# A hybrid attention and state-space block on one core: the split-precision projections as three 256-column matmuls into one sum instead of a 512-column and a 256-column matmul into two

## The chip, the core and the metric

The kernel runs on one NeuronCore of a Trainium2 chip. The core's engines each work through their own instruction list: TensorE (PE, with its weight loads shown apart as PEld), VectorE (DVE), ScalarE (ACT), GpSimd (POOL) and SyncE (SP), which here only issues transfers. Engines meet through semaphores. The metric is the device time of one execution in microseconds (us). The time before is 1421.0 us, the median of three runs (1420.83 to 1421.26).

## The reference

One layer of a hybrid block on a sequence of 256 tokens of width 2048, all in float32:

```
hn   = rms_norm(x, norm_w)
q, k, v, z_a, z_s, xbc, dt_raw, g_a, g_s = split(hn @ w_in)
o_a  = dilated attention of q, k, v (16 heads of 128)  * silu(z_a)
xbc  = silu(causal_depthwise_conv(xbc, 4 taps) + bias)
xs, B, C = split(xbc)          # 4096, 1024 and 1024 columns
y    = state-space scan(xs, softplus(dt_raw), a, B, C) + d_skip * xs
y    = rms_norm(y * silu(z_s), ssm_norm_w)
out  = x + (sigmoid(g_a) * (o_a @ w_attn_branch)
            + sigmoid(g_s) * (y @ w_ssm_branch)) @ w_out
return rms_norm(out, final_norm_w)
```

`w_in` is 2048 x 22592, `w_ssm_branch` 4096 x 2048, `w_attn_branch` and `w_out` 2048 x 2048: 480 tiles of 512 KB, some 252 MB of weights, each read once.

## The kernel before

**Split precision.** Every large product is made of three products in the matmul type fp32r. A weight tile `w` of 128 x 1024 comes in by one transfer and is split into `h` (ACT, L201) and the rest `l = w - h` (DVE, L203). The activations are split in the same way and stand side by side: `XT[:, kt, :256]` is the high part of 256 tokens for the 128 input features of step `kt`, `XT[:, kt, 256:]` the low part. `yT0` holds the same before the tokens' norm factor is known. The product is high x high plus high x low plus low x high.

**Two forms of the product.** In `gemm_b` (gates, v, the branch projections and the last product; L306 to L308) the activations are the stationary operand and 512 weight columns move through the array: three matmuls of 512 columns into one sum for each step and token half. In `gemm_a` (L240, L243) and `gemm_first` (L264, L265) the weights are stationary, 128 x 128, and the tokens move. There `h` is multiplied with all 512 columns of `XT[:, kt, :]`, so that one PSUM bank holds high x high in its first 256 columns and high x low in the last 256, and `l` is multiplied with the 256 high columns and added to the last 256. A projection of 128 output features takes 16 such steps. Three quarters of `w_in`'s columns go this way: the state-space inputs B, C, xs and their gate zs (here called the SSM stage, 31 + 31 + 7 + 7 projections after the first four, which `gemm_first` makes together), `dt` (64 output features wide) and q, k, za of the 16 heads (the attention stage, 48 projections).

**Evacuation.** `evac` (L268) adds the two halves: ACT copies the last 256 columns to SBUF (L270), DVE adds the first 256 from PSUM (L272, or L274 with a factor 0.5). The result goes through the convolution (`conv`: ACT for one tap and the bias, L440, DVE for three taps, L442) and `half_silu` (ACT tanh L280, DVE L281), or straight to q and k. The very first projections (B, C, x, z of group 0 and dt) are made from `yT0` and have to be multiplied with the tokens' factor `rx` afterwards (L276, L398). `rx` comes from ACT's sums of squares (L373), POOL's power (L320), DVE's diagonal (L329), two matmuls that spread it over the partitions (L330) and a DVE copy (L528). The four banks of tag `g` serve all these sums in turn.

**What sets the order.** A scheduler lays out each engine's list at build time. The splitting of weights has high priority; small work (decays, transposes, scan, scores) is put off by `after` and called by `tick` once in each projection, between its first `h` matmul and the next one. One queue, SP's, issues all weight transfers in the order of use.

Of the kernel before, what the change touches and what calls it, by code (L numbers as in the profile page):

```python
# [148 lines left out]
def hybrid_block(ctx: ExitStack, tc: tile.TileContext, wall, xt, x, pk_d, cst_d, fw_d, out):  # L149
# [24 lines left out]
    sel = cst[:, 1408:1536]  # L174
    nw, dsk = pk[:, 256:288], pk[:, 288:320]
    gp.memset(half, -0.5)

    def bank(tag, bufs, name):
# [27 lines left out]

    def split(src, hi, lo, scale=1.0):
        ac.activation(hi, src, AF.Copy, scale=scale)
        if isinstance(scale, float):
# [20 lines left out]
    def gemm_a(tag, xs_of, n_kt=KT, width=P):  # L230
        name = f"{tag[0]}{tag[1]}"
        acc = bank("g", 4, f"ps_{name}") if width == P else bank("m1", 2, f"ps_{name}")
        first = FIRST[tag]
        uk = UNIT // width
        for u in range(n_kt // uk):
            h, l = unit(first + u, (uk, width))
            for kk in range(uk):
                kt = u * uk + kk
                m = xs_of(kt)
                pe.matmul(acc[:width], h[:, kk, :], m, start=(kt == 0), stop=False)  # L240
                if kt == 0:
                    tick()
                pe.matmul(acc[:width, S:], l[:, kk, :], m[:, :S], start=False, stop=(kt == n_kt - 1))  # L243
        return acc

# [3 lines left out]
    def gemm_first(tag, prepare, load_on):  # L249
        name = f"{tag[0]}{tag[1]}"  # L250
        accs = [bank("g", 4, f"ps_{name}_{j}") for j in range(4)]
        for u in range(KT // UB):
            if u % 2 == 0:
                tick()
            for kk in range(UB):
                prepare(u * UB + kk)
            h, l = unit(FIRST[tag] + u, (UB, 512))
            load_on(u)
            for kk in range(UB):
                kt = u * UB + kk  # L260
                m = yT[0][:, kt, :]
                for j, acc in enumerate(accs):
                    js = slice(j * P, (j + 1) * P)
                    pe.matmul(acc, h[:, kk, js], m, start=(kt == 0), stop=False)  # L264
                    pe.matmul(acc[:, S:], l[:, kk, js], m[:, :S], start=False, stop=(kt == KT - 1))  # L265
        return accs

    def evac(acc, out_ap, name, scale=1.0, raw=False):  # L268
        lo = ev.tile([P, S], F32, name=f"lo_{name}", tag="lo", bufs=2)
        ac.activation(lo, acc[:, S:], AF.Copy, scale=scale)  # L270
        if scale == 1.0:
            ve.tensor_tensor(out_ap, acc[:, :S], lo, ALU.add)  # L272
        else:
            ve.scalar_tensor_tensor(out_ap, acc[:, :S], scale, lo, ALU.mult, ALU.add)  # L274
        if raw:
            ve.tensor_tensor(out_ap, out_ap, rx, ALU.mult)  # L276
# [110 lines left out]
    with tc.tile_pool(name="ssm", bufs=2) as sp:  # L387
        def dt_chain(acc):
# [5 lines left out]

            raw, neg, e, z, s, pl, lo, dt, da, ac_t, one = (tmp() for _ in range(11))
# [39 lines left out]
        def conv(acc, ct, out_ap, name, late=False):  # L435
            raw = sp.tile([P, 260], F32, name=f"raw_{name}", tag="raw", bufs=2)
            gp.memset(raw[:, 0:4], 0.0)
            evac(acc, raw[:, 4:], name, raw=late)
            h = ev.tile([P, S], F32, name=f"cv_{name}", tag="eh", bufs=2)
            ac.activation(h, raw[:, 4:], AF.Identity, scale=cw[:, 144 + ct : 145 + ct], bias=cw[:, 192 + ct : 193 + ct])  # L440
            for k in range(3):
                ve.scalar_tensor_tensor(  # L442
                    h, raw[:, 1 + k : 1 + k + S], cw[:, 48 * k + ct : 48 * k + ct + 1], h, ALU.mult, ALU.add
                )
            half_silu(h, out_ap, name)

# [45 lines left out]
        def scan(g, state):  # L492
# [11 lines left out]
            for v, yp in enumerate(yps):  # L504
                u = 2 * g + v
                xs, zs = state["xs"][v], state["zs"][v]
                y1 = sp.tile([P, 2, S], F32, name=f"y1_{u}", tag="y1", bufs=2)
                for i in range(2):
                    t = 2 * u + i
                    ve.scalar_tensor_tensor(  # L510
                        y1[:, i], xs[:, i], dsk[:, t : t + 1], yp[:, i * S : (i + 1) * S], ALU.mult, ALU.add
                    )
                ve.tensor_tensor(y1, y1, zs, ALU.mult)
                ac.activation(xs, y1, AF.Square)
                ve.tensor_tensor(ssq, ssq, xs, ALU.add)
                if u == 8:
                    yT.append(big.tile([P, KT, 2 * S], F32R, name="yT1", tag="yo1"))
                dst = yT[u // 8]
                for i in range(2):
                    t = 2 * u + i  # L520
                    split(y1[:, i], dst[:, t % 16, :S], dst[:, t % 16, S:], scale=nw[:, t : t + 1])

# [4 lines left out]
        with tc.high_priority():  # L527
            ve.tensor_copy(rx, spread(r_x, "x")[:, :S])  # L528
            ve.tensor_scalar(cw, pk[:, 16:256], 0.5, None, ALU.mult)
        for c in range(4):  # L530
            after(1 + 2 * c, lambda c=c: norm_x(c))

        for g in range(GROUPS):
# [12 lines left out]
            for t in range(4 * g, 4 * g + 4):  # L546
# [12 lines left out]
                if i == 0:  # L559
                    state["zs"].append(sp.tile([P, 2, S], F32, name=f"zs{u}", tag="zs", bufs=3))  # L560
                zh = ev.tile([P, S], F32, name=f"zh{t}", tag="eh", bufs=2)
# [8 lines left out]
    with tc.tile_pool(name="att", bufs=2) as ap:  # L570
# [55 lines left out]
        def mix(h, pT, za):  # L626
# [5 lines left out]
            ve.tensor_tensor(o, ops[:, :S], za, ALU.mult)  # L632
            split(o, oaT[:, h, :S], oaT[:, h, S:])

        for h in range(NH):
            q, k = (ap.tile([P, S], F32, name=f"{n}T{h}", tag=f"{n}T", bufs=2) for n in "qk")
            for n, d in (("q", q), ("k", k)):
                evac(project((n, h)), d, f"{n}{h}")
            p = ap.tile([P, 384], F32, name=f"p{h}", tag="p", bufs=2)
# [4 lines left out]
            after(S_LAG, lambda a=(h, q, k, p): scores(*a))  # L644
            zh = ev.tile([P, S], F32, name=f"zah{h}", tag="eh", bufs=2)
            evac(project(("za", h)), zh, f"za{h}", scale=0.5)
            half_silu(zh, za, f"za{h}")

# [92 lines left out]
```

## Time and profile before

| what | value |
|---|---|
| median of three runs | 1421.0 us |
| span of the profiled execution, first to last instruction | 1419.2 us |
| PE busy | 1406.4 us, 99%, 7404 matmul passes |
| DVE busy | 920.5 us, 65% |
| ACT busy | 760.2 us, 54% |
| granted PE clock | 0.999 |
| HBM read | 268.86 MB, 191 GB/s over the span |

The profiled execution's span is 1.8 us below the median of the timed runs, which have a little around the span. A matmul's recorded duration overlaps the next one's, so a matmul's cost on PE is read as the distance from its start to the start of the next, called its slot below. A float32 matmul (not fp32r) shows as two passes.

### The profile page before, as it was taken

What the parts mean: (1) busy time and instruction counts of PE and PEld (TensorE: products, weight loads), DVE (VectorE), ACT (ScalarE), POOL (GpSimd) and SP (SyncE); (2) the same over time, 40 slices, a digit from 0 to 9 for tenths busy, and PEclk for the clock granted to TensorE, in tenths of its full rate; (3) what the DMA queues carried; (4) which work ended last, traced back from release to release, by engine and by line L of the source; (5) the groups of instructions that cost most, each with busy time, mean ns of one, the idle gap of its engine ahead of it and who ended that gap; (6) DMA issues with size and microseconds to landing.
All of it is one profiled execution on the core that took longest, in us unless ns stands there. A gap on an engine that the chain in (4) does not pass through costs nothing.

```text
span 1419.2 us, 19641 instructions
## 1 busy us (share of the span) xinstructions
PE 1406.4 (99%) x7404; PEld 1194.6 (84%) x7404; DVE 920.5 (65%) x1336; ACT 760.2 (54%) x1170; POOL 9.6 (1%) x63
## 2 busy tenths in 40 slices
PE   9999999999999999999999999999999999999997
PEld 7788888888888888888888888888888888888886
DVE  5978888877787888644444446666666654455654
ACT  6656766747575757444533334454544544444443
POOL 0000000000000000000000000000000000000000
PEclk9999999999999999999999999999999999999999
DMA  8566656566656665566566666555555557666663
GB/s 338 183 205 222 197 174 208 169 208 201 189 169 208 194 186 183 167 195 195 187 193 194 192 193 191 176 169 175 170 173 176 168 177 280 193 192 180 191 192 121
DMA packets 77759, 272.31 MB, mean 192 GB/s; under 512 B 8736, under 2 KB 9184, under 8 KB 77024
## 3 DMA queue, kind: packets, MB, share of 16 engines
q1 hardware_dynamic: 77088, 270.01, 60.5%
q8 instruction: 58, 0.95, 0.3%
q10 hardware_dynamic: 576, 1.05, 0.2%
q14 instruction: 37, 0.30, 0.1%
HBM read 268.86 MB, written 2.16 MB: 191 GB/s over the span
## 4 chain that ended last, share of the span: by engine, by line
PE 97%; DVE 1%; issue 0%; DMA 0%; ACT 0%; SPq 0%; POOL 0%; POOLq 0%; DVEq 0%; ACTq 0%
PE ps_xs L240 8%; PE ps_zs L240 8%; PE ps_xs L243 4%; PE ps_q L240 4%; PE ps_zs L243 4%; PE ps_za L240 4%; PE ps_k L240 4%; PE ps_ssm L306 4%; PE ps_ssm L308 4%; PE ps_ssm L307 4%; PE ps_za L243 2%; PE ps_k L243 2%; PE ps_q L243 2%; PE ps_v L306 2%; PE ps_attn L306 2%; PE ps_attn L308 2%
## 5 line engine op out<-in xcount | busy, mean ns | idle before, releaser
L203 DVE TENSOR_TENSOR l<-w,h 128x1024 fp32r<-128x1024 f32 (+1 forms) x481 | 583.1, 1215 | 430.6 <-ACT h L201 428.2
L201 ACT ACTIVATE h<-w 128x1024 fp32r<-128x1024 f32 (+1 forms) x481 | 505.3, 1052 | 573.2 <-PE ps_ssm L308 101.1
L240 PE MATMUL ps_xs<-XT,h 128*128 128x512 f32 x496 | 176.3, 397 | 0.0
L240 PE MATMUL ps_zs<-XT,h 128*128 128x512 f32 x496 | 175.8, 397 | 0.0
L243 PE MATMUL ps_xs<-XT,l 128*128 128x256 f32 x496 | 139.6, 281 | 0.0
L243 PE MATMUL ps_zs<-XT,l 128*128 128x256 f32 x496 | 139.0, 280 | 0.0
L240 PEld LDWEIGHTS ps_zs<-XT,h 128*128 128x128 f32 x496 | 93.1, 188 | 22.6
L240 PEld LDWEIGHTS ps_xs<-XT,h 128*128 128x128 f32 x496 | 93.2, 188 | 22.2
L308 PE MATMUL ps_ssm<-h,yT 128*128 128x512 f32 x256 | 99.6, 389 | 0.0
L307 PE MATMUL ps_ssm<-l,yT 128*128 128x512 f32 x256 | 99.6, 389 | 0.0
L306 PE MATMUL ps_ssm<-h,yT 128*128 128x512 f32 x256 | 99.4, 389 | 0.0
L243 PEld LDWEIGHTS ps_xs<-XT,l 128*128 128x128 f32 x496 | 93.6, 189 | 0.1
L243 PEld LDWEIGHTS ps_zs<-XT,l 128*128 128x128 f32 x496 | 93.6, 189 | 0.0
L240 PE MATMUL ps_q<-XT,h 128*128 128x512 f32 x256 | 90.4, 392 | 0.0
L240 PE MATMUL ps_za<-XT,h 128*128 128x512 f32 x256 | 89.6, 392 | 0.0
L240 PE MATMUL ps_k<-XT,h 128*128 128x512 f32 x256 | 89.6, 391 | 0.0
L243 PE MATMUL ps_q<-XT,l 128*128 128x256 f32 x256 | 74.5, 291 | 0.0
L243 PE MATMUL ps_k<-XT,l 128*128 128x256 f32 x256 | 71.7, 280 | 0.0
L243 PE MATMUL ps_za<-XT,l 128*128 128x256 f32 x256 | 71.7, 280 | 0.0
L240 PEld LDWEIGHTS ps_q<-XT,h 128*128 128x128 f32 x256 | 47.9, 187 | 10.6
L240 PEld LDWEIGHTS ps_k<-XT,h 128*128 128x128 f32 x256 | 47.9, 187 | 10.6
L240 PEld LDWEIGHTS ps_za<-XT,h 128*128 128x128 f32 x256 | 47.9, 187 | 10.6
(235 smaller groups left out, 2553.5 us busy)
## 6 DMA issues: line engine op xcount, KB each, us to landing
w<-in_wall SPq DMA_DIRECT2D x480, 512.0 KB, 3.6
acb<-acum_d SPq DMA_DIRECT2D x32, 256.0 KB, 3.2
th_s<-in_x SPq DMA_DIRECT2D x1, 2048.0 KB, 9.6
fin<-in_x SPq DMA_DIRECT2D x1, 2048.0 KB, 8.1
early<-in_xt SPq DMA_DIRECT2D x7, 256.0 KB, 7.0
fw<-in_fw SPq DMA_DIRECT2D x1, 1024.0 KB, 10.1
out<-fin SPq DMA_DIRECT2D x4, 256.0 KB, 2.9
out<-fin ACTq DMA_DIRECT2D x4, 256.0 KB, 3.2
```

What stands on the lines that cost most here:

```text
L201: ac.activation(h[:, a:b], w[:, a:b], AF.Copy)
L203: eng.tensor_tensor(l[:, a:b], w[:, a:b], h[:, a:b].bitcast(F32), ALU.subtract)
L240: pe.matmul(acc[:width], h[:, kk, :], m, start=(kt == 0), stop=False)
L243: pe.matmul(acc[:width, S:], l[:, kk, :], m[:, :S], start=False, stop=(kt == n_kt - 1))
L306: pe.matmul(accs[i], xh, h, start=(kt == 0), stop=False)
L307: pe.matmul(accs[i], xh, l, start=False, stop=False)
L308: pe.matmul(accs[i], xl, h, start=False, stop=(kt == n_kt - 1))
```

## The change

Each step of a weight-stationary projection becomes three matmuls of 256 columns, `h` with the high tokens, `h` with the low tokens, `l` with the high tokens, all into the same 256 columns of the bank. So there is no second half to add, and `evac` is gone: q and k are one ACT copy from PSUM; the silu gates and the convolution read PSUM directly (ACT once, DVE once or three times); the convolution's zero padding is replaced by shorter taps (253, 254 and 255 columns). The projections of group 0 are multiplied with `rx` straight from PSUM into a `raw` tile. The factor 0.5 that stood in the gate's evacuation moves into the tanh's scale, the norm weights `nwh`, the square and the last split of the attention output.

```diff
@@ gemm_a
-                pe.matmul(acc[:width], h[:, kk, :], m, start=(kt == 0), stop=False)
+                pe.matmul(acc[:width, :S], h[:, kk, :], m[:, :S], start=(kt == 0), stop=False)
                 if kt == 0:
                     tick()
-                pe.matmul(acc[:width, S:], l[:, kk, :], m[:, :S], start=False, stop=(kt == n_kt - 1))
-        return acc
+                pe.matmul(acc[:width, :S], h[:, kk, :], m[:, S:], start=False, stop=False)
+                pe.matmul(acc[:width, :S], l[:, kk, :], m[:, :S], start=False, stop=(kt == n_kt - 1))
+        return acc[:width, :S]
@@ gemm_first
-                    pe.matmul(acc, h[:, kk, js], m, start=(kt == 0), stop=False)
-                    pe.matmul(acc[:, S:], l[:, kk, js], m[:, :S], start=False, stop=(kt == KT - 1))
+                    pe.matmul(acc[:, :S], h[:, kk, js], m[:, :S], start=(kt == 0), stop=False)
+                    pe.matmul(acc[:, :S], h[:, kk, js], m[:, S:], start=False, stop=False)
+                    pe.matmul(acc[:, :S], l[:, kk, js], m[:, :S], start=False, stop=(kt == KT - 1))
...
-    def evac(acc, out_ap, name, scale=1.0, raw=False):
...
-    def half_silu(h, out_ap, name):
+    def silu(src, th_scale, out_ap, name):
         th = ev.tile([P, S], F32, name=f"th_{name}", tag="th", bufs=2)
-        ac.activation(th, h, AF.Tanh)
-        ve.scalar_tensor_tensor(out_ap, th, 1.0, h, ALU.add, ALU.mult)
+        ac.activation(th, src, AF.Tanh, scale=th_scale)
+        ve.scalar_tensor_tensor(out_ap, th, 1.0, src, ALU.add, ALU.mult)
@@ dt_chain
-            ac.activation(lo, acc[:SH, S:], AF.Copy)
-            ve.tensor_tensor(raw, acc[:SH, :S], lo, ALU.add)
-            ve.tensor_tensor(raw, raw, rx[:SH], ALU.mult)
+            ve.tensor_tensor(raw, acc, rx[:SH], ALU.mult)
@@ conv
-            gp.memset(raw[:, 0:4], 0.0)
-            evac(acc, raw[:, 4:], name, raw=late)
+            if late:
+                raw = sp.tile([P, S], F32, name=f"raw_{name}", tag="raw", bufs=2)
+                ve.tensor_tensor(raw, acc, rx, ALU.mult)
+                acc = raw
-            ac.activation(h, raw[:, 4:], AF.Identity, scale=..., bias=...)
+            ac.activation(h, acc, AF.Identity, scale=..., bias=...)
             for k in range(3):
+                d = 3 - k
                 ve.scalar_tensor_tensor(
-                    h, raw[:, 1 + k : 1 + k + S], cw[...], h, ALU.mult, ALU.add
+                    h[:, d:], acc[:, : S - d], cw[...], h[:, d:], ALU.mult, ALU.add
                 )
-            half_silu(h, out_ap, name)
+            silu(h, 1.0, out_ap, name)
@@ zs gate
-                evac(acc, zh, f"z{t}", scale=0.5, raw=t == 0)
-                half_silu(zh, state["zs"][-1][:, i], f"z{t}")
+                silu(acc, 0.5, state["zs"][-1][:, i], f"z{t}")
@@ attention
-                evac(project((n, h)), d, f"{n}{h}")
+                ac.activation(d, project((n, h)), AF.Copy)
...
-            evac(project(("za", h)), zh, f"za{h}", scale=0.5)
-            half_silu(zh, za, f"za{h}")
+            silu(project(("za", h)), 0.5, za, f"za{h}")
```

Over the whole program PE's list grows from 7013 to 9077 rows, DVE's shrinks from 1173 to 1091, ACT's from 1054 to 958, POOL's from 68 to 20, and SP's 531 stay.

How the lists move, at three places. First, PE inside a projection of the SSM stage (`ps_xs` is the sum in PSUM, `XT` the tokens, `h` and `l` the weight parts); before:

```order
L240 MATMUL ps_xs_831<-XT,h_856 128x512 [waits Activation_49]
L243 MATMUL ps_xs_831<-XT,l_857 128x256 [waits DVE_49]
L240 MATMUL ps_xs_831<-XT,h_856 128x512
L243 MATMUL ps_xs_831<-XT,l_857 128x256
L240 MATMUL ps_xs_831<-XT,h_856 128x512
```

and in the change:

```order
L241 MATMUL ps_xs_896<-XT,h_899 128x256 [waits Activation_49]
L244 MATMUL ps_xs_896<-XT,h_899 128x256
L245 MATMUL ps_xs_896<-XT,l_900 128x256 [waits DVE_49]
L241 MATMUL ps_xs_896<-XT,h_899 128x256
L244 MATMUL ps_xs_896<-XT,h_899 128x256
L245 MATMUL ps_xs_896<-XT,l_900 128x256
```

A step of two matmuls has become one of three, in unbroken order.

Second, PE at the start of the first gate projection (`ps_gs`), right behind the dt projection; `rb_x` are the two matmuls that spread the norm factor. Before:

```order
L243 MATMUL ps_dt_352<-yT_84,l_354 64x256
L330 MATMUL rb_x<-diag_x,cst 128x128 [waits DMAHW6_49,DVE_49]
L306 MATMUL ps_gs_0_487<-h_498,yT_84 128x512 [waits PE_49,Activation_49]
L306 MATMUL ps_gs_1_488<-h_498,yT_84 128x512 [waits PE_49]
L330 MATMUL rb_x<-diag_x,cst 128x128 [waits DVE_49]
L307 MATMUL ps_gs_0_487<-l_499,yT_84 128x512 [waits DVE_49]
```

and in the change:

```order
L245 MATMUL ps_dt_417<-yT_85,l_419 64x256
L323 MATMUL rb_x<-diag_x,cst 128x128 [waits DMAHW6_49,DVE_49]
L323 MATMUL rb_x<-diag_x,cst 128x128 [waits DVE_49]
L299 MATMUL ps_gs_0_552<-h_563,yT_85 128x512 [waits DVE_49,Activation_49]
L300 MATMUL ps_gs_0_552<-l_564,yT_85 128x512
L301 MATMUL ps_gs_0_552<-h_563,yT_85 128x512
```

The gate's first matmul now waits for DVE too, and stands behind both matmuls of the norm factor.

Third, DVE in the same place. Before:

```order
L203 TENSOR_TENSOR l_499<-w_273,h_498 128x1024 [waits DMAHW7_49,DVE_49,Activation_49]
L203 TENSOR_TENSOR l_517<-w_514,h_516 128x1024 [waits DMAHW0_49,DVE_49,Activation_49]
L528 COPY rx<-rb_x 128x256 [waits PE_49]
L397 TENSOR_TENSOR early<-ps_dt_352,early 64x256 [waits Activation_49]
L203 TENSOR_TENSOR l_545<-w_542,h_544 128x1024 [waits DMAHW1_49,DVE_49,Activation_49]
L276 TENSOR_TENSOR raw_B_400<-raw_B_400,rx 128x256 [waits DVE_49]
L276 TENSOR_TENSOR raw_C_414<-raw_C_414,rx 128x256
L378 TENSOR_TENSOR early<-early,rx 128x1024 x3
```

and in the change:

```order
L204 TENSOR_TENSOR l_564<-w_314,h_563 128x1024 [waits DMAHW7_49,PE_49,Activation_49]
L521 COPY rx<-rb_x 128x256 [waits PE_49]
L204 TENSOR_TENSOR l_582<-w_579,h_581 128x1024 [waits DMAHW0_49,Activation_49]
L429 TENSOR_TENSOR raw_B_482<-ps_first_0_120,rx 128x256 [waits DVE_49]
L429 TENSOR_TENSOR raw_C_492<-ps_first_1_121,rx 128x256
L389 TENSOR_TENSOR early<-ps_dt_417,rx 64x256
L371 TENSOR_TENSOR early<-early,rx 128x1024 x4
L204 TENSOR_TENSOR l_610<-w_607,h_609 128x1024 [waits DMAHW1_49,Activation_49]
```

The accumulators of B and C (`ps_first_0`, `ps_first_1`) are read for the first time behind `rx`, and the third `l` of the gate has moved from ahead of the token scaling (L378, now L371) to behind all four parts of it.

More of the change, by code (lines that the diff above doesn't have):

```diff
@@ L174, in hybrid_block @@
     sel = cst[:, 1408:1536]
-    nw, dsk = pk[:, 256:288], pk[:, 288:320]
+    dsk = pk[:, 288:320]
     gp.memset(half, -0.5)
+    nwh = lead.tile([P, 32], F32, name="nwh", tag="nwh")
     def bank(tag, bufs, name):
@@ L205, in unit, with split @@
         return h.rearrange("p (k m) -> p k m", k=k), l.rearrange("p (k m) -> p k m", k=k)
-    def split(src, hi, lo, scale=1.0):
-        ac.activation(hi, src, AF.Copy, scale=scale)
-        if isinstance(scale, float):
+    def split(src, hi, lo, scale=None):
+        ac.activation(hi, src, AF.Copy, scale=1.0 if scale is None else scale)
+        if scale is None:
             ve.tensor_tensor(lo, src, hi.bitcast(F32), ALU.subtract)
@@ L263, in gemm_first @@
                     js = slice(j * P, (j + 1) * P)
-                    pe.matmul(acc, h[:, kk, js], m, start=(kt == 0), stop=False)
-                    pe.matmul(acc[:, S:], l[:, kk, js], m[:, :S], start=False, stop=(kt == KT - 1))
-        return accs
-    def evac(acc, out_ap, name, scale=1.0, raw=False):
[L269 to L276, printed above, removed]
-    def half_silu(h, out_ap, name):
+                    pe.matmul(acc[:, :S], h[:, kk, js], m[:, :S], start=(kt == 0), stop=False)
+                    pe.matmul(acc[:, :S], h[:, kk, js], m[:, S:], start=False, stop=False)
+                    pe.matmul(acc[:, :S], l[:, kk, js], m[:, :S], start=False, stop=(kt == KT - 1))
+        return [acc[:, :S] for acc in accs]
+    def silu(src, th_scale, out_ap, name):
         th = ev.tile([P, S], F32, name=f"th_{name}", tag="th", bufs=2)
-        ac.activation(th, h, AF.Tanh)
-        ve.scalar_tensor_tensor(out_ap, th, 1.0, h, ALU.add, ALU.mult)
+        ac.activation(th, src, AF.Tanh, scale=th_scale)
+        ve.scalar_tensor_tensor(out_ap, th, 1.0, src, ALU.add, ALU.mult)
     def gemm_b(tag, x_of, n_kt=KT, held=None):
@@ L393, in tmp @@
                 return dts[:, len(used) - 1, :]
-            raw, neg, e, z, s, pl, lo, dt, da, ac_t, one = (tmp() for _ in range(11))
-            ac.activation(lo, acc[:SH, S:], AF.Copy)
-            ve.tensor_tensor(raw, acc[:SH, :S], lo, ALU.add)
-            ve.tensor_tensor(raw, raw, rx[:SH], ALU.mult)
+            raw, neg, e, z, s, pl, dt, da, ac_t, one = (tmp() for _ in range(10))
+            ve.tensor_tensor(raw, acc, rx[:SH], ALU.mult)
             ve.tensor_scalar(raw, raw, pk[:SH, 320:321], None, ALU.add)
@@ L513, in scan @@
                 ve.tensor_tensor(y1, y1, zs, ALU.mult)
-                ac.activation(xs, y1, AF.Square)
+                ac.activation(xs, y1, AF.Square, scale=0.5)
                 ve.tensor_tensor(ssq, ssq, xs, ALU.add)
@@ L529, in hybrid_block @@
             ve.tensor_scalar(cw, pk[:, 16:256], 0.5, None, ALU.mult)
+            ve.tensor_scalar(nwh, pk[:, 256:288], 0.5, None, ALU.mult)
         for c in range(4):
@@ L560, in hybrid_block @@
                     state["zs"].append(sp.tile([P, 2, S], F32, name=f"zs{u}", tag="zs", bufs=3))
-                zh = ev.tile([P, S], F32, name=f"zh{t}", tag="eh", bufs=2)
-                evac(acc, zh, f"z{t}", scale=0.5, raw=t == 0)
-                half_silu(zh, state["zs"][-1][:, i], f"z{t}")
+                if t == 0:
+                    zr = sp.tile([P, S], F32, name="raw_z", tag="raw", bufs=2)
+                    ve.tensor_tensor(zr, acc, rx, ALU.mult)
+                    acc = zr
+                silu(acc, 0.5, state["zs"][-1][:, i], f"z{t}")
                 if t == 0:
@@ L632, in mix @@
             ve.tensor_tensor(o, ops[:, :S], za, ALU.mult)
-            split(o, oaT[:, h, :S], oaT[:, h, S:])
+            split(o, oaT[:, h, :S], oaT[:, h, S:], scale=0.5)
         for h in range(NH):
```

8 lines of the change are left out of this document (3 added, 5 removed).

## The prediction

> **What bounds the kernel now.** I read the page's first part and the waits of PE first, to see whether PE ever stands still, then PE's timeline, because a busy PE says nothing of how fast it goes.
>
> ```profile
> PE 1406.4 (99%) x7404; PEld 1194.6 (84%) x7404; DVE 920.5 (65%) x1336; ACT 760.2 (54%) x1170; POOL 9.6 (1%) x63
> PE 97%; DVE 1%; issue 0%; DMA 0%; ACT 0%; SPq 0%; POOL 0%; POOLq 0%; DVEq 0%; ACTq 0%
> PE ps_gs L307 <- DVE l L203: 2.1, 3, 1.1
> PE warm L343 <- POOL raw_C L437: 1.3, 1, 1.3
> PE ps_first L264 <- ACT h L201: 1.0, 2, 0.8
> L203 DVE TENSOR_TENSOR l<-w,h 128x1024 fp32r<-128x1024 f32 (+1 forms) x481 | 583.1, 1215 | 430.6 <-ACT h L201 428.2
> ```
>
> PE is busy 99% of the span and 97% of the chain that ended last; in the whole program it waits 4.4 us for others. DVE's largest group sits idle for 430.6 us waiting for ACT, so neither has too much to do. Relief for them can give back at most the waits of PE on them, 2.1 and 1.0 us, both in the first 62 us. So the change is decided by what it does to PE's slots (start to start). Two stretches of the timeline show a step before; columns are start, duration, engine, line, operation.
>
> ```profile
> 1000.21 0.39 PE L240 MATMUL ps_q<-XT,h 128*128 128x512 f32 x1
> 1000.21 0.19 PEld L243 LDWEIGHTS ps_q<-XT,l 128*128 128x128 f32 x1
> 1000.43 0.28 PE L243 MATMUL ps_q<-XT,l 128*128 128x256 f32 x1
> 1000.44 0.19 PEld L240 LDWEIGHTS ps_q<-XT,h 128*128 128x128 f32 x1
> 1000.55 0.39 PE L240 MATMUL ps_q<-XT,h 128*128 128x512 f32 x1
> ...
> 1003.33 0.39 PE L240 MATMUL ps_k<-XT,h 128*128 128x512 f32 x1
> ...
> 101.46 0.40 PE L240 MATMUL ps_zs<-XT,h 128*128 128x512 f32 x1
> 106.66 0.39 PE L240 MATMUL ps_zs<-XT,h 128*128 128x512 f32 x1
> ...
> 400.38 0.40 PE L240 MATMUL ps_zs<-XT,h 128*128 128x512 f32 x1
> 405.69 0.40 PE L240 MATMUL ps_zs<-XT,h 128*128 128x512 f32 x1
> ```
>
> In attention 9 steps take 1003.33 - 1000.21 = 3.12 us, 347 ns each: some 230 for the wide matmul and 117 for the narrow one. In the SSM stage I find two speeds, whole projections long: 15 steps in 5.20 us (347 each, from 101.46) and in 5.31 us (354 each, from 400.38). Most are of the slower kind; I take 352 as the stage's mean. Under each matmul, from its start on, the weights of the next are loaded.
>
> **The change part by part.** *The number of steps:* 76 later SSM projections and 48 of attention have 16 steps each, 1216 and 768; the first four have 64, dt 16; 2064 together, and 2064 matmuls and loads are added. The columns that move stay 768 a step. So the question is what three narrow slots cost against a wide and a narrow one. Two places of this trace answer it from two sides. The first is dt, whose weights are 64 wide:
>
> ```profile
> 29.57 0.39 PE L240 MATMUL ps_dt<-yT,h 128*64 128x512 f32 x1
> 29.79 0.28 PE L243 MATMUL ps_dt<-yT,l 128*64 128x256 f32 x1
> 29.91 0.39 PE L240 MATMUL ps_dt<-yT,h 128*64 128x512 f32 x1
> ...
> 34.67 0.39 PE L240 MATMUL ps_dt<-yT,h 128*64 128x512 f32 x1
> L243 PEld LDWEIGHTS ps_dt<-yT,l 128*64 128x64 f32 x16 | 2.1, 134 | 0.0
> ```
>
> 15 steps in 5.10 us are 340 ns for 768 columns, so 113.3 for each 256 columns: with a short load (134 ns recorded) the slot is the moving alone. That is the lower bound. The other is the start, where four accumulators are fed in turn with full 128-wide weights and narrow matmuls follow one another, as they will everywhere after the change:
>
> ```profile
> 12.27 0.64 PE L265 MATMUL ps_first<-yT,l 128*128 128x256 f32 x4
> 12.75 1.09 PE L264 MATMUL ps_first<-yT,h 128*128 128x512 f32 x4
> 13.68 0.63 PE L265 MATMUL ps_first<-yT,l 128*128 128x256 f32 x4
> 14.15 1.09 PE L264 MATMUL ps_first<-yT,h 128*128 128x512 f32 x4
> 15.08 0.64 PE L265 MATMUL ps_first<-yT,l 128*128 128x256 f32 x4
> ```
>
> Four narrow slots take 0.48 and 0.47 us, 117.5 to 120 each. So a 128-wide load under a narrow matmul isn't hidden whole: it adds 4 to 7 ns to the 113.3. A wide one hides it better: 230 against 226.7 in attention. The change puts three loads where two were, and all three under narrow matmuls. I take 118 a slot, 354 a step, with 117 and 120 (351 and 360) as the ends. The sum lies between +7 and +2 ns a step: attention 768 x 7 = +5.4 us; SSM 1216 x 2 = +2.4; the first four projections 64 x (354 - 350) = +0.3, where 350 is (14.15 - 12.75) / 4; dt 0. Together +8.1 us. At 117 it is 768 x 4 - 1216 x 1 = +1.9, at 120 it is 768 x 13 + 1216 x 8 + 64 x 10 = +20.4.
>
> A rule speaks against the change in another way. The Trainium skill ("TensorE: Matmul & The Clock Gate", section "Back-to-back issue gap") gives a matmul a fixed 2.5 ns beside its columns; two narrow ones for a wide one would then cost 2064 x 2.5 = 5.2 us more. The dt rows don't show it: their wide slot (29.57 to 29.79) and narrow slot (29.79 to 29.91) are as 2 to 1, so by the trace this term is 0 and what counts is the load.
>
> *Is the second load of the same weights saved?* The gates, v and branch projections already use one stationary operand in two matmuls in a row (L306 and L307 both load the high activations):
>
> ```profile
> L307 PEld LDWEIGHTS ps_ssm<-l,yT 128*128 128x128 f32 x256 | 48.1, 188 | 9.9
> L306 PEld LDWEIGHTS ps_ssm<-h,yT 128*128 128x128 f32 x256 | 48.1, 188 | 9.8
> ```
>
> Both are loaded 256 times, 188 ns each; it isn't saved, and I cost it in full. Adding into columns that were written 256 columns ago is nothing new either: before, `l` follows on the last 256 columns of `h`'s bank at that distance.
>
> *Evacuation.* ACT loses a copy and DVE an addition for each projection. This is worth nothing while PE is the bound (above). The sums stay in their bank longer: before until the addition, now until the third tap or the gate's product. With four banks in turn a bank is wanted again three projections later, some 16 x 350 x 3 ns = 17 us. The cover is that DVE and ACT run close behind; gone, PE would stop at a projection's start. I take 0.
>
> *The first gate.* This is the one place where a wait moves, and the order at the second and third place of the change shows it.
>
> ```profile
> 18.42 0.38 SPq L367 DMA_DIRECT2D th_s<-in_x  x1
> th_s<-in_x SPq DMA_DIRECT2D x1, 2048.0 KB, 9.6
> 29.48 0.42 DVE L272 TENSOR_TENSOR raw_C<-ps_first,lo_C 128x256 f32<-128x256 f32 x1
> 29.92 1.91 ACT L373 ACTIVATE th_s<-th_s 128x2048 f32<-128x2048 f32 x1
> 35.36 2.35 DVE L203 TENSOR_TENSOR l<-w,h 128x1024 fp32r<-128x1024 f32 x2
> 36.63 0.50 PE L307 MATMUL ps_gs<-l,yT 128*128 128x512 f32 x1 [0.23 <-DVE l L203]
> 37.63 0.41 DVE L528 COPY rx<-rb_x 128x256 f32<-128x256 f32 x1
> 40.10 3.48 DVE L378 TENSOR_TENSOR early<-early,rx 128x1024 f32<-128x1024 f32 x3
> 46.24 0.50 PE L307 MATMUL ps_gs<-l,yT 128*128 128x512 f32 x1 [1.15 <-DVE l L203]
> 55.45 0.50 PE L307 MATMUL ps_gs<-l,yT 128*128 128x512 f32 x1 [0.76 <-DVE l L203]
> ```
>
> Before, the additions at 29.5 free the two banks and PE is at its third gate matmul at 36.63, so as if it had begun at 36.2. Now the banks come free only with the products by `rx`. ACT no longer has the copies of L270, which wait for PE's last matmul, ahead of its squares, so these can start when `th_s` lands, 18.42 + 9.6 = 28.0, 1.9 us earlier; then PE's last dt matmul at 35.0 sets `rx`, at some 35.7. Behind it come one `l` (1.15) and the first product (0.4): the gate begins at 37.6, 1.4 us late. After that DVE is late with the third `l`, which now stands behind four token scalings (4 x 1.15 = 4.6), and with the fifth, behind ten splits of XT. Walking the list with these durations I get PE waits of 0.5, 2.2 and 0.4 in place of the 1.15, 0.76 and 0.23 shown: 1 us more, +2 us in all, rounded down. Bounds: 0, if DVE's shorter list catches up, and 4.5, if the late start and the new waits come with none of the old ones saved.
>
> The sum: 1419.2 + 8.1 + 2 = 1429.3 us of span; with the 1.8 us that the median lies above the span, 1431 us.
>
> **The rivals.** *Faster: the load hides after all.* If three equal slots let each load end in time, as in dt, a step is 340: -7 x 768 - 12 x 1216 - 10 x 64 = -20.6 us, +2 for the gate, 1402 us. It pays from slots below 116.6 on (the mean step before, 350, divided by 3). For it speaks that the two speeds of the SSM stage look like a matter of how loads and matmuls fall together, which a new rhythm may change. Against it stand the runs of four narrow matmuls at 117.5 to 120. A rule would give it: the Trainium skill, same page, section "LDWEIGHTS (loading the stationary operand)", has 128 columns load in 128 / 1.2 = 107 ns, less than a narrow slot. The narrow slots of 117 with a full load, against 113 with a half one, don't bear that out.
>
> *No change: the repeated weights cost less.* If the middle matmul of a step, whose weights are those in the array, has a 113.3 slot, a step is 349.3: 768 x 2.3 - 1216 x 2.7 = -1.5 us, and with the gate's 2 us about 1421.5. The rows of L306 and L307 say that the load is done, not that it costs the same as any.
>
> *Much slower: PE can't take in a load and a matmul every 118 ns for 1000 us.* Now it takes two pairs in 347. If the pace were 125 a pair, a step would be 375: 768 x 28 + 1216 x 23 + 64 x 25 = +51 us, 1474. Against it: eight transposes in a row at a pair every (1.03 - 0.27) / 7 = 109 ns; but eight are few.
>
> ```profile
> 130.62 1.03 PE L482 MATMUL xtp<-cst,xs 128*128 128x128 f32 x8
> ```
>
> **How the numbers follow.** About 0.2% (2.8 us) is what a measurement of this kernel can tell from no change. My forecast, slots of 117 to 120 and the gate, has 0.67, and its own range is 1423 to 1446; a little of it, at 117 and with no loss at the gate, counts as no change. The repeated-weights rival has 0.13, the hidden load 0.14, the pace 0.06. So faster 0.14, within 0.2% 0.17, slower 0.69. The range that should hold 8 in 10 leaves out the pace and most of the hidden load: 1414 to 1444.
>
> **What would show it.** Right: PE still above 98% busy, the steps of q at 351 to 360 ns, PEld near 9470 loads with 188 each, DVE some 50 us less busy (129 additions of 0.42, as in the row of L272), ACT nearly as much, the first gate beginning near 37.6 us. The hidden load: steps of 340 and PEld rows no shorter. Repeated weights: the slot between L241 and L244 or L244 and L245 shorter than the others. Pace: steps above 365 with gaps put down to issue. Wrong in another way: waits of PE for DVE or ACT at the start of projections, which would mean that banks are held too long.

## The result: 1444.2 us, 1.6% slower

The changed kernel takes 1444.2 us (median of 4 runs, 1444.13 to 1444.30) against 1421.1 us for the kernel before (4 runs beside it). The ratio is 1.016, with a 95% interval of 1.0146 to 1.0175. The forecast was 1431 us with a range of 1414 to 1444: slower was right, the loss is 23 us where 10 were expected, and the time lies 0.2 us above the range. The profiled execution has a span of 1442.4 us and a granted clock of 0.998 (0.999 before).

The page of the changed kernel, its first part and two of its groups (total busy time, then the mean of one in ns):

```profile
PE 1427.5 (99%) x9468; PEld 1308.3 (91%) x9468; DVE 877.4 (61%) x1208; ACT 726.3 (50%) x1073; POOL 6.0 (0%) x15
L204 DVE TENSOR_TENSOR l<-w,h 128x1024 fp32r<-128x1024 f32 (+1 forms) x481 | 584.1, 1216 | 490.4 <-ACT h L202 489.7
L244 PEld LDWEIGHTS ps_xs<-XT,h 128*128 128x128 f32 x496 | 95.2, 192 | 0.1
```

DVE is 43.1 us less busy than before (920.5 - 877.4) and ACT 33.9 us (760.2 - 726.3). Neither gain arrives in the span: DVE's largest group now stands idle for 490.4 us instead of 430.6. PE is still busy 99% of the time, and busy 21.1 us longer. The second matmul of `h` (L244) has its load like any other, 192 ns recorded where the loads of the wide matmul (L240) had 188 before.

PE's slots in attention, timeline of the changed kernel (start, duration, engine, line):

```profile
1000.01 0.28 PE L244 MATMUL ps_q<-XT,h 128*128 128x256 f32 x1
1000.13 0.28 PE L245 MATMUL ps_q<-XT,l 128*128 128x256 f32 x1
1000.25 0.28 PE L241 MATMUL ps_q<-XT,h 128*128 128x256 f32 x1
...
1002.29 0.28 PE L245 MATMUL ps_q<-XT,l 128*128 128x256 f32 x1
```

Nineteen slots take 2.28 us: each is 120 ns, whether the weights are new or those of the matmul ahead. A step is 360 ns. It is so in every projection with 128-wide weights from the SSM stage on, but for the first one or two steps behind other work.

The loss by place, from the starts of the first matmul of each stage. Before:

```profile
82.74 0.39 PE L240 MATMUL ps_xs<-XT,h 128*128 128x512 f32 x1
564.96 0.40 PE L306 MATMUL ps_gs<-h,XT 128*128 128x512 f32 x1
852.76 0.39 PE L240 MATMUL ps_q<-XT,h 128*128 128x512 f32 x1
1143.92 0.58 PE L306 MATMUL ps_ga<-h,XT 128*128 128x512 f32 x1
```

After (with the first and last high matmul of dt):

```profile
30.94 0.28 PE L241 MATMUL ps_dt<-yT,h 128*64 128x256 f32 x1
36.05 0.28 PE L241 MATMUL ps_dt<-yT,h 128*64 128x256 f32 x1
86.09 0.28 PE L241 MATMUL ps_xs<-XT,h 128*128 128x256 f32 x1
578.96 0.40 PE L299 MATMUL ps_gs<-h,XT 128*128 128x512 f32 x1
866.70 0.28 PE L241 MATMUL ps_q<-XT,h 128*128 128x256 f32 x1
1167.30 0.58 PE L299 MATMUL ps_ga<-h,XT 128*128 128x512 f32 x1
```

| stage | later at its end, us | lost in it, us | forecast, us |
|---|---|---|---|
| first four projections (dt began at 29.57) | 1.37 | 1.4 | 0.3 |
| dt and the first gates | 3.35 | 2.0 | 2 |
| SSM stage | 14.0 | 10.65 | 2.4 |
| last gate, v, branch product | 13.94 | -0.1 | 0 |
| attention | 23.38 | 9.4 | 5.4 |
| the rest, to the end of the span | 23.2 | -0.2 | 0 |

The waits of PE at the first gate and the rows around it, changed kernel:

```profile
PE ps_gs L299 <- DVE raw_B L429: 2.1, 1, 2.1
PE ps_gs L300 <- DVE l L204: 1.9, 1, 1.9
```

```profile
29.15 1.91 ACT L366 ACTIVATE th_s<-th_s 128x2048 f32<-128x2048 f32 x1 [3.88 <-DMA th_s<-in_x]
38.51 0.42 DVE L429 TENSOR_TENSOR raw_B<-ps_first,rx 128x256 f32<-128x256 f32 x1
39.08 0.47 PE L299 MATMUL ps_gs<-h,yT 128*128 128x512 f32 x1 [2.07 <-DVE raw_B L429]
52.92 0.50 PE L300 MATMUL ps_gs<-l,yT 128*128 128x512 f32 x1 [1.87 <-DVE l L204]
```

The gate begins when `raw_B` has freed its bank, and loses once more when `l` comes late behind the token scalings. These two stand in place of three smaller waits, and no projection waits for its bank later on.

### The profile page after: what moved, and what is told of

It reads as the page before. It is cut to its first block, busy times and chain, and to the rows that moved or that the text cites. A ratio compares the mean times of both kernels' runs of the same rounds, so it can differ in the third digit from the quotient of the medians.

```text
span 1442.4 us, 23370 instructions
## 1 busy us (share of the span) xinstructions
PE 1427.5 (99%) x9468; PEld 1308.3 (91%) x9468; DVE 877.4 (61%) x1208; ACT 726.3 (50%) x1073; POOL 6.0 (0%) x15
## 4 chain that ended last, share of the span: by engine, by line
PE 97%; DVE 1%; DMA 0%; issue 0%; SPq 0%; ACT 0%; POOLq 0%; DVEq 0%; POOL 0%
PE ps_xs L244 4%; PE ps_xs L241 4%; PE ps_zs L244 4%; PE ps_zs L241 4%; PE ps_zs L245 4%; PE ps_xs L245 4%; PE ps_ssm L299 4%; PE ps_ssm L301 4%; PE ps_ssm L300 4%; PE ps_za L245 2%; PE ps_k L244 2%; PE ps_k L241 2%; PE ps_za L244 2%; PE ps_k L245 2%; PE ps_za L241 2%; PE ps_q L245 2%
## 5 line engine op out<-in xcount | busy, mean ns | idle before, releaser
L204 DVE TENSOR_TENSOR l<-w,h 128x1024 fp32r<-128x1024 f32 (+1 forms) x481 | 584.1, 1216 | 490.4 <-ACT h L202 489.7
L244 PE MATMUL ps_xs<-XT,h 128*128 128x256 f32 x496 | 140.9, 284 | 0.0
L241 PE MATMUL ps_xs<-XT,h 128*128 128x256 f32 x496 | 140.6, 283 | 0.0
L244 PE MATMUL ps_zs<-XT,h 128*128 128x256 f32 x496 | 140.5, 283 | 0.0
L241 PE MATMUL ps_zs<-XT,h 128*128 128x256 f32 x496 | 140.4, 283 | 0.0
L244 PEld LDWEIGHTS ps_xs<-XT,h 128*128 128x128 f32 x496 | 95.2, 192 | 0.1
L241 PEld LDWEIGHTS ps_xs<-XT,h 128*128 128x128 f32 x496 | 95.2, 192 | 0.1
L241 PEld LDWEIGHTS ps_zs<-XT,h 128*128 128x128 f32 x496 | 95.2, 192 | 0.0
L244 PEld LDWEIGHTS ps_zs<-XT,h 128*128 128x128 f32 x496 | 95.2, 192 | 0.0
L244 PE MATMUL ps_q<-XT,h 128*128 128x256 f32 x256 | 75.2, 294 | 0.0
L241 PE MATMUL ps_za<-XT,h 128*128 128x256 f32 x256 | 72.5, 283 | 0.0
L244 PE MATMUL ps_k<-XT,h 128*128 128x256 f32 x256 | 72.5, 283 | 0.0
L244 PE MATMUL ps_za<-XT,h 128*128 128x256 f32 x256 | 72.5, 283 | 0.0
```

What stands on the lines that cost most here:

```text
L204: eng.tensor_tensor(l[:, a:b], w[:, a:b], h[:, a:b].bitcast(F32), ALU.subtract)
L241: pe.matmul(acc[:width, :S], h[:, kk, :], m[:, :S], start=(kt == 0), stop=False)
L244: pe.matmul(acc[:width, :S], h[:, kk, :], m[:, S:], start=False, stop=False)
```

## The experiments

The theory after the result: the loss is the slots, three narrow matmuls with full loads at 120 ns each, plus 2 us at the first gate. The rivals: adding twice into the same columns slows PE, holding banks longer or reading PSUM directly costs time, the repeated load is special. The runs of the split, the evacuation, the single-matmul series and the early copy have the kernel before beside them at 1421.4 us.

### Only the split of the matmul

Against the kernel before:

```diff
-                pe.matmul(acc[:width], h[:, kk, :], m, start=(kt == 0), stop=False)
+                pe.matmul(acc[:width, :S], h[:, kk, :], m[:, :S], start=(kt == 0), stop=False)
                 if kt == 0:
                     tick()
+                pe.matmul(acc[:width, S:], h[:, kk, :], m[:, S:], start=False, stop=False)
```

The same in `gemm_first`. Both sums and the old evacuation stay.

> The kernel before, with nothing changed but the wide matmul of each step: it becomes two of 256 columns, still into two halves of the bank, and the evacuation stays. Load theory (a slot is as long as a full weight load, 120 ns, when loads follow one another under narrow matmuls): all slots 120, steps 360, attention +9.5 us and the SSM stage +10.5, first four +0.6: about 1441.5 us, and the first gate not late. Sum theory (adding three times into the same 256 columns is what stretches the slots): slots back at 113 to 117, about 1411 to 1423 us. Evacuation theory (the late readers of PSUM stretch them): likewise 1411 to 1423 us.

Measured: 1442.3 us (4 runs, 1441.46 to 1443.46), ratio 1.0147 (1.0132 to 1.0162). Its waits of PE and its slots:

```profile
PE ps_gs L309 <- DVE l L203: 2.4, 1, 2.4
```

```profile
1000.04 0.28 PE L240 MATMUL ps_q<-XT,h 128*128 128x256 f32 x1
1000.28 0.28 PE L244 MATMUL ps_q<-XT,l 128*128 128x256 f32 x1
```

Two slots take 0.24 us, so 120 again, with two sums and the old evacuation. This edit alone makes 20.9 of the 23.1 us. From the starts of the stages in its trace, the SSM stage loses 10.65 us, attention 9.44 and the first four projections 1.4, as in the changed kernel, and the first gates nothing (0.1 us less). So neither one sum for all nor the direct reading is the cause of the slots, and what is left, some 2 us, is what the first gate loses.

### Only the evacuation

Against the changed kernel:

```diff
-                pe.matmul(acc[:width, :S], h[:, kk, :], m[:, :S], start=(kt == 0), stop=False)
+                pe.matmul(acc[:width], h[:, kk, :], m, start=(kt == 0), stop=False)
                 if kt == 0:
                     tick()
-                pe.matmul(acc[:width, :S], h[:, kk, :], m[:, S:], start=False, stop=False)
-                pe.matmul(acc[:width, :S], l[:, kk, :], m[:, :S], start=False, stop=(kt == n_kt - 1))
+                pe.matmul(acc[:width, S:], l[:, kk, :], m[:, :S], start=False, stop=(kt == n_kt - 1))
```

The same in `gemm_first`. PE does what it did before; the second half of each sum is not read, so the two low products are left out of the output.

> The changed kernel with the matmuls of before (512 and 256 columns, two halves) but the new evacuation, which reads the first half alone; the second half, high x low and low x high, is computed and left out of the result. Load theory: steps of 347 and 353 as before, only the first gate late by 2 us: 1423 us. Evacuation theory: most of the 23 us is here, 1440 us or more. If relief of DVE and ACT were worth something, below 1421 us.

Measured: 1421.6 us (10 runs), ratio 1.0003 (0.9994 to 1.0013). Its waits of PE:

```profile
PE ps_gs L297 <- DVE raw_B L427: 2.2, 1, 2.2
PE ps_gs L298 <- DVE l L204: 0.6, 1, 0.6
```

The first later projection starts 2.4 us late (85.11 against 82.74 us), as the gate's terms ask. By the start of attention only 0.6 us of it is left: the SSM stage took 1.7 us less, although its PE work is that of before. That was not foreseen (1423 us was expected); it is taken up again under the rhythm below. The evacuation as a whole, the late gate included, changes the time by nothing that can be measured.

### Slots by themselves, ten series of 48 matmuls

The kernel before (1489.9 us with the series, one run), with series placed between the SSM stage and v, whose sums nobody reads. Weights are slices of one tile, the moving data are slices of `XT`:

```diff
+        for j in range(NP):
+            pe.matmul(pa[:, :256], wt(j), mv(j, 256), **flags(j))
...
+        for j in range(NP):
+            pe.matmul(pc[:, :256], wt(0), mv(j, 256), **flags(j))
...
+        for j in range(NP):
+            pe.matmul(pd[:64, :256], wt(j, 64), mv(j, 256), **flags(j))
...
```

In this order: 256 columns into the same place (L592), into the two halves of the bank in turn (L596), with the same weights each time (L599), with weights 64 and 96 wide (L602, L605), then 320, 128 and 512 columns with full weights (L608, L611, L614), and 256 and 512 columns with the roles exchanged, as in the gates (L617, L620).

> The kernel before with ten series of 48 matmuls put in behind the SSM stage, whose sums nobody reads; each has a line of its own, so its slot can be read. Weights from a tile, tokens move. Load theory: 256 columns into one place 120 ns; alternating between two halves 120; the same weights each time 120; weights 96 wide below 117, 64 wide 113; 320 columns 142 (the moving alone, 320 x 0.443); 128 columns 110 to 120 (the load alone); 512 columns 227 to 236; roles exchanged (tokens stationary, a weight tile moves) 120 at 256 and 227 at 512 columns. Sum theory: alternating halves 113. Repeated-weights theory: the same weights 113. Together some 75 us more.

From one profiled execution, the first row of each series in the timeline:

```profile
603.03 0.28 PE L592 MATMUL pa<-XT,pw 128*128 128x256 f32 x1
608.67 0.28 PE L596 MATMUL pb<-XT,pw 128*128 128x256 f32 x1
614.30 0.28 PE L599 MATMUL pc<-XT,pw 128*128 128x256 f32 x1
619.93 0.28 PE L602 MATMUL pd<-XT,pw 128*64 128x256 f32 x1
625.55 0.28 PE L605 MATMUL pf<-XT,pw 128*96 128x256 f32 x1
631.15 0.31 PE L608 MATMUL pg<-XT,pw 128*128 128x320 f32 x1
638.20 0.22 PE L611 MATMUL pi<-XT,pw 128*128 128x128 f32 x1
643.50 0.44 PE L614 MATMUL pj<-XT,pw 128*128 128x512 f32 x1
654.79 0.28 PE L617 MATMUL pk__6532<-pw,XT 128*128 128x256 f32 x1
660.55 0.40 PE L620 MATMUL pl__6581<-pw,XT 128*128 128x512 f32 x1
```

From one start to the next lie 48 slots. That gives 117 to 118 for the same place, halves in turn and the same weights each time (5.64, 5.63, 5.63 us), 117 for 64 and 96 wide (5.62, 5.60), 147 for 320 columns, 110 for 128 columns, 235 for 512 and 120 for exchanged roles at 256; with exchanged roles at 512 columns it is 233 (to 671.75, not shown).

Three things follow. Where the sum goes costs nothing, and loading the same weights again saves nothing: both rivals fall. And full loads can follow one another at 110 ns (L611), so "a load takes 120 ns" is no explanation. Beside the moving alone, taken as 113.3 ns for each 256 columns as in dt, a matmul with a full load costs more at every width from 256 columns on: 117 against 113, 147 against 142 (320 columns), 235 against 227 (512). So the wide matmul pays as well, and not only the narrow one. But the series does not give 120: in it slots of 115 to 120 alternate, and 64-wide weights are hardly faster (117), unlike dt. So a row of single matmuls does not yet reproduce the kernel.

### The kernel's own shape, by itself

Eleven series of 32 steps in the same place (1544.9 us in all, one run), in the kernel's form: the weights from the kernel's own pools, wide and narrow or three narrow, high and low tokens in turn.

```diff
+        for j in range(NS):
+            pe.matmul(pa, wt(sh, j), mv(j), **fl(j, True, False))
+            pe.matmul(pa[:, S:], wt(sl, j), mv(j)[:, :S], **fl(j, False, True))
...
+        for j in range(NS):
+            pe.matmul(pb[:, :S], wt(sh, j), mv(j)[:, :S], **fl(j, True, False))
+            pe.matmul(pb[:, :S], wt(sh, j), mv(j)[:, S:], **fl(j, False, False))
+            pe.matmul(pb[:, :S], wt(sl, j), mv(j)[:, :S], **fl(j, False, True))
...
```

In this order: wide and narrow (L597), three narrow (L601), three wide with the roles exchanged (L607), wide and narrow with weights from other tiles (L612) and from there 32 bytes on (L616), wide and narrow with weights 64 wide (L620), three narrow with weights 64 wide (L624), two wide and then two narrow (L629), and twice the first form again. Their sums are not read either.

> The kernel before with eleven series of 32 steps put in behind the SSM stage, which copy the steps of the kernel: a 512-column and a 256-column matmul, weights 128 wide from tiles of the weight pool; three of 256 columns; three of 512 with the roles exchanged as in the gates; the first form with tiles elsewhere, with weights shifted by 32 bytes, and with weights 64 wide; three narrow ones 64 wide; the first form in the order wide, wide, narrow, narrow; the first form again, before and behind two transposes. Load theory as revised (the moving needs 340 ns a step, each full-width load adds 0 or one quantum of 6.7 ns): 347 or 353, 351 to 360, 680, 347 or 353 three times or 340 if the shift avoids a clash, 340 with 64-wide weights in both forms, 347 to 360. Theory that the width of the load has no part in it (as the 64-wide series of the first probe hinted with 117 ns): the 64-wide forms as slow as the full ones, 350 and 352.

From one profiled execution, the first rows of eight series:

```profile
594.70 0.39 PE L597 MATMUL pa<-XT,sh 128*128 128x512 f32 x1
605.99 0.28 PE L601 MATMUL pb<-XT,sh 128*128 128x256 f32 x1
617.51 0.40 PE L607 MATMUL pc<-sh,XT 128*128 128x512 f32 x1
639.30 0.39 PE L612 MATMUL pd<-XT,qh 128*128 128x512 f32 x1
650.39 0.39 PE L616 MATMUL pf<-XT,qh 128*128 128x512 f32 x1
661.65 0.39 PE L620 MATMUL pg<-XT,sh 128*64 128x512 f32 x1
672.56 0.28 PE L624 MATMUL pi<-XT,sh 128*64 128x256 f32 x1
683.45 0.40 PE L629 MATMUL pj<-XT,sh 128*128 128x512 f32 x1
```

32 steps of wide and narrow take 11.29 us (353 each), of three narrow 11.52 (360), of three wide with roles exchanged 21.79 (681, which is 3 x 227), of wide and narrow from other tiles 11.09 (347), shifted by 32 bytes 11.26 (352), 64 wide 10.91 (341), and three narrow 64 wide 10.89 (340). Not shown: two wide, then two narrow, 348 a step; the first form again 353, also behind two transposes.

So here the kernel's numbers are back, as means: single slots of the three narrow matmuls go from 117 to 124. Three narrow matmuls with 128-wide weights take 360 a step; make the weights 64 wide, and the same form takes 340, the third matmul and its load included. So in this form the extra time hangs on the full width of the weights. Weights 64 wide also halve the rows of the sum that is written; the load and the writing are not separated here. And wide and narrow take 347 in one series and 353 in another, without any wait.

### A copy that frees the first banks early

Against the changed kernel, in the convolution of the first projections:

```diff
-                ve.tensor_tensor(raw, acc, rx, ALU.mult)
+                ac.activation(raw, acc, AF.Copy)
+                ve.tensor_tensor(raw, raw, rx, ALU.mult)
```

> The changed kernel, but the first four projections are copied out of PSUM by ACT before the norm factor is known and multiplied in SBUF. If the first gate's late start comes from banks held until the factor is known, the 2.1 us wait of PE on raw_B goes and the total falls by 1.5 to 2.5 us, to about 1442 us; all steps stay at 360. If DVE is the bound there anyway, the wait only moves to a later weight rest and the total stays at 1444.

Measured: 1443.0 us (4 runs, 1442.74 to 1443.40), ratio to the kernel before 1.0151 (1.0135 to 1.0168), 1.2 us below the changed kernel. Its waits of PE:

```profile
PE ps_gs L300 <- DVE l L204: 1.9, 2, 1.1
PE ps_gs L299 <- ACT th_s L307: 1.1, 1, 1.1
```

The wait for `raw_B` is gone, and some 1.1 of the gate's 2.0 us come back (the first later projection starts at 84.82 instead of 86.09; 0.14 of these 1.27 us come from the first four). Half of the wait moved on to ACT's own list. So the gain is a little less than the 1.5 to 2.5 us expected, and the intervals of the two ratios overlap; it is the traces that show it. The price of the late banks is small, and giving it back needs the very copies that the change took away.

### The rhythm: other places for the small work

The SSM stage before has whole projections at 347 and at 353 ns a step, and the series above had both speeds for one form, without a wait. Both are means, and 353 is one throughout: single steps at that speed go 350, 350 and 361 in turn, those at the other either 347 each or 350 and 343 in turn. In the trace of before the speed changes for the most part where other matmuls stand between the projections: behind the scan (L500) with the product of C and B (L449) right after it the steps are at 353 all six times, behind the transposes of `xs` (L482) at 347 in most. Two constants set how many projections later this work is called. If a rhythm, once begun, is kept, moving the work must change the time of the SSM stage, with not a matmul more or less.

The first of two kernels, against the kernel before, puts C x B a projection later, away from the scan:

```diff
-DT_LAG, CB_LAG, TURN_LAG, GT_LAG, Y_LAG, S_LAG, M_LAG = 2, 3, 2, 1, 6, 2, 2
+DT_LAG, CB_LAG, TURN_LAG, GT_LAG, Y_LAG, S_LAG, M_LAG = 2, 4, 2, 1, 6, 2, 2
```

> The kernel before, with the group's C x B product put off by one projection (its lag 4 instead of 3), so that it no longer stands right behind the scan. Before, whole projections run at 346.7 ns a step or at 353.3, and which of the two changes only where other work is put in between. Theory of a kept rhythm (the speed of a projection is set by what it was entered with, not by its operands): the places at which the speed changes move, and the time goes up or down by up to 5 us, 1416 to 1424 us. Theory of place (the speed belongs to the tile's address or to the work of DVE and ACT at the time): the same projections stay slow and the time stays within 1 us of 1421.

Measured: 1419.35 us (10 runs, 1418.42 to 1421.16), the kernel before beside it 1421.7, ratio 0.9987 (0.9977 to 0.9997).

In it the steps behind C x B are at 347, but those behind the transposes, now called at that speed, at 353 until the scan. So the second kernel moves the transposes too, close ahead of the scan:

```diff
-DT_LAG, CB_LAG, TURN_LAG, GT_LAG, Y_LAG, S_LAG, M_LAG = 2, 3, 2, 1, 6, 2, 2
+DT_LAG, CB_LAG, TURN_LAG, GT_LAG, Y_LAG, S_LAG, M_LAG = 2, 4, 5, 1, 6, 2, 2
```

> The kernel before with two lags changed: the C x B product behind the scan by one projection (4 instead of 3) and the eight transposes of xs one projection ahead of the scan (5 instead of 2). With the first of these alone the projections behind the C x B product ran at 346.7 ns a step and those behind the transposes at 353.3. Theory of a kept rhythm: the transposes still switch to the slow rhythm, but only one projection per group is left before the scan and the product switch back, so two projections of 16 steps x 6.7 ns in each of seven groups are won on top: about 1.5 us less than with the one lag, 1417 to 1418.5 us. If the rhythm has to do with the place in the group and not with what stood before, no more is won: 1419 to 1420 us.

Measured: 1417.5 us (8 runs, 1417.29 to 1417.87), the kernel before beside it 1421.5, ratio 0.9973 (0.9962 to 0.9983). One group of the SSM stage, before:

```profile
406.37 2.82 PE L500 MATMUL yp<-gt,xdt 128*64 128x256 f32 x32
409.12 0.70 PE L449 MATMUL cbp<-ct,bt 128*128 128x256 f32 x2
415.29 0.40 PE L240 MATMUL ps_zs<-XT,h 128*128 128x512 f32 x1
415.64 0.40 PE L240 MATMUL ps_zs<-XT,h 128*128 128x512 f32 x1
415.99 0.40 PE L240 MATMUL ps_zs<-XT,h 128*128 128x512 f32 x1
416.35 0.40 PE L240 MATMUL ps_zs<-XT,h 128*128 128x512 f32 x1
420.59 0.40 PE L240 MATMUL ps_zs<-XT,h 128*128 128x512 f32 x1
```

and in the second kernel:

```profile
398.14 1.03 PE L482 MATMUL xtp<-cst,xs 128*128 128x128 f32 x8
405.12 2.82 PE L500 MATMUL yp<-gt,xdt 128*64 128x256 f32 x32
413.16 0.59 PE L449 MATMUL cbp<-ct,bt 128*128 128x256 f32 x2
419.14 0.39 PE L240 MATMUL ps_xs<-XT,h 128*128 128x512 f32 x1
424.34 0.39 PE L240 MATMUL ps_xs<-XT,h 128*128 128x512 f32 x1
```

The 15 steps from 415.29 take 5.30 us before (353 each), those from 419.14 in the second kernel 5.20 (347 each), where C x B stands a projection behind the scan and the transposes a projection ahead of it. I count the stretches of a projection of the SSM stage with eight steps or more and no other matmul between; three steps take 1060 ns in those at 353 and 1040 in those at 347. Before, 53 are at 353 and 23 at 347; in the first kernel 31 and 45, in the second 17 and 59. At 16 steps of 6.7 ns, 22 and 36 fewer at 353 are 2.4 and 3.9 us; measured are 2.3 and 4.0, and in the traces the SSM stage has become 2.4 and 3.8 us shorter and no other stage by more than 0.3. The kernel with the evacuation alone has 38 and 38: 15 fewer are 1.6 us, so nearly all of the 1.7 us that it won there. The second kernel beats both kernels of this case, by 4.0 and 26.7 us, with the computation of before.

The second kernel's time is the one expected, but not in the way expected. Behind the transposes, entered at 347, its steps stay at 347; it is the projection behind the scan that runs at 353, until C x B. Over the four traces (before, these two and the evacuation alone) the scan alone is always followed by 353 and C x B alone always by 347, but the transposes, entered at 347, by 353 in the first kernel (five times) and by 347 in the second (five times), and the scan with C x B, entered at 347, by 353 before (five times) and by 347 twice in the kernel with the evacuation alone. So a speed, once begun, is kept, and which work is called where changes it. What in it decides is not shown. It need not be PE's list alone, since DVE's and ACT's work moves with it, and the operands' place may matter too: of the series above, the one shifted by 32 bytes had 352 a step right behind one of 347.

### The same constant in the changed kernel

```diff
-DT_LAG, CB_LAG, TURN_LAG, GT_LAG, Y_LAG, S_LAG, M_LAG = 2, 3, 2, 1, 6, 2, 2
+DT_LAG, CB_LAG, TURN_LAG, GT_LAG, Y_LAG, S_LAG, M_LAG = 2, 4, 2, 1, 6, 2, 2
```

> The changed kernel with the same product put off by one projection (lag 4). If three narrow matmuls with three full loads always fall into the slowest rhythm, whatever they were entered with, every step stays at 360 ns and the time within 1 us of 1444. If the changed kernel is slow because of the rhythm it happened to be entered with, some projections come down to 347 or 353 and the time falls by 2 us or more.

Measured: 1445.2 us (4 runs, 1443.86 to 1446.03), ratio to the kernel before 1.0166 (1.0152 to 1.0180): no gain over the changed kernel's 1444.2. Its stretches of eight steps and more are all at 360, as in the changed kernel and the one with the split alone. In none of these three did the three narrow matmuls take another speed, so this move of the small work had nothing to win.

## Why the prediction was right in the cause and wrong in the size

- **The bound.** Right. PE set the time in the kernels compared here, and DVE's 43 and ACT's 34 us of relief were worth nothing, as costed: the split without them takes the changed kernel's time less the gate (first experiment), and they alone take the time of before (second).
- **The count of steps and loads.** Right: 2064 matmuls and loads more, 9468 in all. The repeated weights are loaded and paid for like any others, in the kernel and in the series with the same weights (L599).
- **The slot of 118 ns: the step that failed.** The sum took 118, between the ends 117 and 120; the kernel has 120, so a step of 360 instead of 354. The forecast's own sum for that end, +20.4 us with the first four, is nearly what came: 10.65 + 9.4 in the two stages and 1.4 in the first four. The error is in how the 118 was got. The nine runs of four narrow matmuls at the start that stand without a wait have a mean of 118.0, so the reading was no slip; but slot by slot four of them begin at 113 to 118, behind a wide matmul, and go on with 119 or 120, 120, 120, while in the others all slots stay at 113 to 119. A run of four does not say where a long row settles. The value of a long row, 120, stood in those four runs, and no row of the trace before was long enough to decide.
- **Attention and SSM apart.** Both kinds of step end at 360. Attention, mostly at 347 before, loses 9.4 us instead of 5.4 (768 x 13 = 10.0, less what its few slower projections lose less); SSM, at some 351 before and not at 352, loses 10.65 instead of 2.4 (1216 x 8.8). That a wide matmul hides the load better (230 against 226.7) was read from steps at 347; in the steps of before at 353 the wide slots are 233, 236 and 241 and the narrow ones 113, 117 and 120. The forecast saw the two speeds and used them as a mean; that they can be set was missed.
- **dt.** Right: 15 steps in 5.11 us (30.94 to 36.05), 340.7 against 340 before, with a matmul more in each. This also answers the rule of the Trainium skill ("TensorE: Matmul & The Clock Gate", "Back-to-back issue gap"): that 2.5 ns, which the section gives for a matmul by itself, would make it 342.5 with a third matmul. The trace does not show it.
- **The first four.** 1.4 us lost instead of 0.3: 0.4 more wait for ACT's first `h` (1.43 against 1.0 us), 0.6 by slots of 120, and some 0.3 unexplained.
- **The first gate.** Right in mechanism and size: 2.0 us, with a wait for `raw_B` at its start and one for a late `l` further on, 2.1 and 1.9 us; three waits of 0.5, 2.2 and 0.4 were forecast for the latter. The gate began at 39.08 and not 37.6, but 1.37 of that came from the stage ahead. ACT's squares began at 29.15 and not 28.0, but `rx` waited for PE's last dt matmul anyway, as forecast.
- **Evacuation at nothing.** Right (second experiment, 1.0003). After the first gate PE waits for no bank.
- **The rivals.** The hidden load (340 a step) came only with 64-wide weights. The Trainium skill's 107 ns for a full load (same page, "LDWEIGHTS (loading the stationary operand)") is close to the 110 ns of the 128-column series (L611), where the moving alone would be 57 by dt's rate; what doesn't follow is that such a load is hidden under a moving of 113. The repeated weights and the pace beyond 125 did not come.
- **The range.** Its upper end left out what the forecast's own term allowed: 1421 + 20.4 + 2 is 1443.4 and, with 4.5 at the gate, 1446. The forecast's own range had that end, the 8-in-10 range cut it.

Not settled: why a matmul with full weights costs 7 ns more than its moving in a row of narrow ones. The runs show that in the kernel's form it hangs on the width of the weights (64 wide: none), and not on where the sum goes or on the weights being new; they do not show which resource is short, nor whether it is the load or the 128 rows of the sum. Nor is it settled why the single-matmul series had 117 with 64-wide weights too, or why the transposes and the scan start one rhythm or the other.

## What to carry to other kernels

Where PE is the bound, a split of a wide matmul into narrow ones can cost time although the columns stay the same, as here with weights 128 wide (and not with dt's 64): price the new step from the longest unbroken row of that shape in the trace, slot by slot, or measure a series in the kernel's own form, before counting what other engines save. If equal steps run at two speeds, look at what stands on PE ahead of each; here moving some small work by a projection or three gave 4 us for nothing. A range should keep the end that the least certain row allows.

## What the runs showed of the hardware that was not expected

- **Steps settle into few patterns.** Where nothing stands between, a step of 768 columns settles in these kernels at a mean of 340 (dt), 346.7, 353.3 or 360 ns. No single step takes 353: that mean is 350, 350 and 361 in turn. In the series other means came too, 348 and 352, so the four are no fixed grid; what makes the patterns is open.
- **The rhythm is kept.** A projection goes on at the speed of the one ahead until something else stands between its matmuls, other work of PE or a break in their order. Changing only where the small work is called took 1421.5 to 1417.5 us.
- **Exchanged roles pay nothing in the kernel's form.** Three 512-column matmuls with the tokens stationary take 681 a step, 227 each, twice dt's 113.3, with the same full loads (188 ns recorded); the kernel's gates have the same 227. In the single-matmul series it was 233.
